# A chunk inverse ahead of the attention, with twelve gate projections between its steps

## The chip, the cores and the metric

The kernel runs on one core of a Trainium2 chip. The metric is the device time of the whole program in microseconds (us), here the median of three runs. Engines are named as the profile names them: PE is TensorE's matmul, PEld its weight load, DVE is VectorE, ACT is ScalarE, POOL is GpSimd, SP is SyncE, which here only issues transfers.

## The reference

One layer of a streaming encoder on 1,024 tokens of 1,024 channels in float32: token mixing, cross attention into 256 memory tokens, and a retrieval over 16,384 single-neuron experts, each with a residual. What the change touches is the token mixing:

```
proj = rmsnorm(x) @ w_in          # sb_q, sb_k, sb_v | g_q, g_k, g_v | g_z | g_b, g_a | gate_sb, gate_gdn
o_sb = stick_breaking_attention(sb_q, sb_k, sb_v)            # 8 heads x 64, causal
q, k, v = silu(causal_dwconv([g_q, g_k, g_v]));  q, k = l2norm(q), l2norm(k)
A  = strict_lower(beta * (k k^T) * decay)                    # per chunk and head, 4 heads x 128
u, w = (I + A)^-1 [beta v, beta k exp(g)]                    # the chunk inverse
for each chunk: v' = u - w S;  o = (q S) + (q k^T * decay) v';  S = decayed S + k^T v'
o_g = rmsnorm(o) * silu(g_z)
merged = sigmoid(gate_sb) * (o_sb @ w_sb_up) + sigmoid(gate_gdn) * (o_g @ w_gdn_up)
out = merged @ w_mix_out
```

The retrieval takes 128 experts per token: their rows of `peer_u` (dot products with the token), a GELU with gates, and the weighted sum of their rows of `peer_v`.

## The kernel before, in words

The tokens go through in three groups of 256, 384 and 384, called g0, g1 and g2 here. `token_mixing(g)`, the cross attention and the routing (which picks the experts) follow each other for each group; g2's routing is followed by dense products over all experts (`dense_h`, line 975), which replace the retrieval for the last tokens. The retrieval of the earlier tokens runs beside all of that from g1 on: line 778 (POOL) gathers 128 expert rows of 4 KB per instruction by an indirect transfer into a `row` buffer; for `peer_u` line 794 (DVE) multiplies the rows by the tokens and sums them (called a u reduce here; a second instruction reads out the sum), for `peer_v` either line 823 (PE, groups of eight small matmuls into `ac`) or line 83 (DVE, into `y`) adds them up.

The order on each engine is set when the program is built, by a scheduler that goes by its own estimate of times, under the dependencies, the buffers and the lifetimes of the memory pools; the engines then work through their lists strictly in order. Code written one after the other is thus interleaved where buffers allow.

Inside `token_mixing` (lines 440 to 550) the steps before are: the norm; twelve projections of 128 columns each for g_q, g_k, g_v with their short convolution (`gc` buffers); beta and decay; SiLU (line 487); l2norm of q and k (line 493 on PE and line 83 `gc<-gc,sq` on DVE); twelve projections for the attention ("SB projections", into `qT`, `kT` and, transposed, `vN`); the attention itself, `stick`, in blocks of 128 queries and 128 keys, two generators (heads 0 to 3 and 4 to 7) in turn; twenty gate projections, whose sigmoid goes to DRAM; the chunk inverse; the scan over the chunks; then the output projections (first DVE line 571, `gr`).

Every projection (`proj`, lines 226 to 240) loads a 512 KB tile of weights, splits it in two parts (ACT line 77 `wh<-raw`, DVE line 89 `wl<-raw,wh`) and runs 24 matmuls (line 223) into one of two PSUM buffers `pj`. One block pair of the attention (called a pair here: one generator, one key block) has one ACT instruction `sh<-z` (line 80), by which pairs can be counted; g0 has 6 pairs, g1 24, g2 42. `pool.tensor_tensor(after, ...)` is line 295.

A chunk's inverse (`Chunk.inverse`, lines 373 to 415) first prepares A (lines 326 to 365, up to `X` in line 377), then doubles diagonal blocks over six levels, each a chain PE (line 379/393/395), ACT (`K`, `E`), DVE or ACT (`X`, line 399), with masks by POOL (line 370). The two or three chunks of a group run in turn. Chunk 0 uses the PSUM tile `z`, chunk 1 `acc`, chunk 2 the two `pj` buffers, the same that the projections use.

The pools: `pn`/`ta` hold `kT`, `vN`, `qT` and the attention's buffers; `d2` holds the inverse's. They are opened one after the other, so what is opened second reuses the memory of the first.

Of the kernel before, what the change touches and what calls it, by code (L numbers as in the profile page):

```python
# [8 lines left out]
F32 = mybir.dt.float32  # L9
# [11 lines left out]
P = 128  # L21
D = 1024
# [29 lines left out]
def block_kernel(ctx: ExitStack, tc: tile.TileContext, x_t, mem_t, gains, cst, sel, eye, w_in, conv, a_log,  # L52
# [22 lines left out]
    # ---- small helpers  # L75
# [9 lines left out]
    def split(hi, lo, src, scale=1.0, eng=vec):  # L85
        """src * scale = hi + lo, both in the tensor engine's fast float32 format."""
        copy(hi, src, scale)
        if scale == 1.0:
            eng.tensor_tensor(lo, src, hi, op=OP.subtract)  # L89
        else:  # L90
            stt(lo, src, scale, hi, OP.mult, OP.subtract)
# [10 lines left out]
    def acc_keep(o, lhsT, rhs, start):  # L102
        """Matmul onto a bank that is read between its accumulation steps."""
        pe.matmul(o, lhsT=lhsT, rhs=rhs, start=start, stop=True, skip_group_check=True)
# [13 lines left out]
    def mix(a, b, ratio):  # L118
        """Steps of a and b in turn, ratio of a for each of b."""
# [21 lines left out]
    # ---- constants  # L141
# [43 lines left out]
    # ---- scratch in DRAM  # L185
# [15 lines left out]
    # ---- building blocks  # L201
    def norm_t(hi, lo, tmp, xs, gi, n, keep=None):
        """RMSNorm over the partitions and tiles of xs(k), [P, n] each, split in two parts."""
# [22 lines left out]
    def proj(w, col0, ncol, hi, lo, n, kt=KD, share=0):  # L226
        """Yields (tile index, product) for each 128 columns of w, transposed: [columns, tokens]. GpSimd splits
        every share-th tile of w."""
# [35 lines left out]
    # ---- stick-breaking attention of one 128-query block, four heads at a time, keys on partitions  # L264
    def stick(tmp, kT, vN, qT, sbo, e, qb, t0):
# [4 lines left out]
        for kb in range(qb, -1, -1):  # L270
# [6 lines left out]
            # softplus; for large z the logarithm is z itself  # L277
# [26 lines left out]
    # ---- gated delta net over one 128-token chunk, four heads together  # L304
    class Chunk:
# [67 lines left out]
        def inverse(self):  # L373
            """Inverse of (I + A) by doubling of diagonal blocks, and its transpose; AT holds -A transposed."""
# [26 lines left out]
            # keys and values with tokens on partitions  # L401
# [15 lines left out]
        def scan(self, S, S2, o):  # L417
            """Recurrence over chunks."""
# [17 lines left out]
    def token_mixing(g, t0, T, x1_where, result):  # L436
# [3 lines left out]
        with ExitStack() as eo:  # L440
# [11 lines left out]
            # gated delta net: projections, short convolution  # L452
# [9 lines left out]
            # beta and decay logits  # L462
# [35 lines left out]
            yield  # L498
            with ExitStack() as es:
# [21 lines left out]
                if not last:  # L521
                    sp.dma_start(k_sc[:, :, t0:t1], kT[:, :, t0:t1])
                    sp.dma_start(v_sc[:, t0 // P:t1 // P], vN[:, t0 // P:t1 // P])
                for qb in range(t0 // P, t1 // P):
                    run(*[stick(tmp, kT, vN, qT, sbo, e, qb, t0) for e in range(2)])

            oT = qkv[0]
            with ExitStack() as es:
                tmp = open_pool(f"d2{g}", 2, where=es)
                # output gate and branch gates wait in DRAM  # L530
                n = 0
                for o, m in ((O_Z, 512), (O_GS, 2048)):
                    for i, ps in proj(w_in, o, m, xh, xl, T, share=SH_Z):
                        e = po.tile([P, T], F32, name="ev", bufs=2)
                        sigmoid(e, ps)
                        if o == O_Z:
                            vec.tensor_mul(e, e, ps)
                        sp.dma_start(gate_sc[g, n, :, :T], e)
                        n += 1
                chunks = []  # L540
                for c in range(NB):
                    cc = slice(c * P, (c + 1) * P)
                    chunks.append(Chunk(tmp, c, qkv[0][:, :, cc], qkv[1][:, :, cc], qkv[2][:, :, cc], bT[:, cc], gT[:, cc]))
                run(*[ch.inverse() for ch in chunks])
                for c, ch in enumerate(chunks):
                    cur = chunk_no[0] % 2
                    chunk_no[0] += 1
                    ch.scan(state[cur], state[1 - cur], oT[:, :, c * P:(c + 1) * P])
# [86 lines left out]
    def routing(g, x1, t0, T, where, kept=None):  # L635
        """Returns the pool that choose() goes on with, and by block the best scores and keys."""
# [62 lines left out]
    def choose(tmp, tv, ti):  # L699
        """The sixteen best sums per head of one 128-token block. A pair (a, b) of ranks can be among them  # L700
        only with (a + 1) * (b + 1) <= 16: a < 4 with all b, or b < 4."""
# [21 lines left out]
        # gate: softmax over the chosen sixteen (the first is the largest)  # L723
# [7 lines left out]
        # position -> ranks -> expert  # L731
# [43 lines left out]
    # ---- retrieval by gathering expert rows  # L775
# [6 lines left out]
    def retrieve_u(blk, keep):  # L782
        """Expert activations of one block; tokens on partitions, one slot per gather."""
# [25 lines left out]
    def retrieve_v(blk, keep):  # L809
        """Weighted sum of expert rows, residual and final norm; slots on partitions, one token per gather."""  # L810
# [22 lines left out]
    def retrieve_y(blk, keep):  # L833
        """The same with tokens on partitions, one slot per gather."""
# [26 lines left out]
    def finish(y, ps, r0):  # L861
        """Final norm of 64 tokens, 32 w + p: quarter d of the channels of token (w, p) is y[32 d + p, w]."""
# [11 lines left out]
    # ---- retrieval by dense products over all experts, for the last tokens  # L874
    def choose_t(p2, tv, ti):
        """Keys and gates of one block with the slots on partitions."""
# [8 lines left out]
    def spread(px_, sel3, b):  # L885
        """Gates as a matrix: g_sc[c, i, r, t] is the gate of token 32 * c + t for expert 128 * r + i, zero if not
# [236 lines left out]
```

## Time and profile before

| | |
|---|---|
| median of three runs | 3813.43 us (3813.3 to 3814.75) |
| span of the profiled execution | 3821.6 us, 8.2 us (0.2%) above that median |
| PE, PEld busy | 3402.2 us (89%), 2852.3 us (75%) |
| DVE, ACT, POOL busy | 2852.1 us (75%), 1624.2 us (43%), 1993.3 us (52%) |
| indirect gathers (queue q0) | 671 MB, 49.4% of sixteen DMA engines' span |
| other transfers (queue q1) | 426 MB, 36.4% |

Busy times overlap between the engines. A matmul's end is modelled, so a PE that is busy throughout need not be at its peak; PEld, the weight loads beside it, is read together with it. The profile gives no time of its own for the profiled execution beside the span; the span is taken as that time.

### The profile page before, as it was taken

What the parts mean: (1) busy time and instruction counts of PE and PEld (TensorE: products, weight loads), DVE (VectorE), ACT (ScalarE), POOL (GpSimd) and SP (SyncE); (2) the same over time, 40 slices, a digit from 0 to 9 for tenths busy, and PEclk for the clock granted to TensorE, in tenths of its full rate; (3) what the DMA queues carried; (4) which work ended last, traced back from release to release, by engine and by line L of the source; (5) the groups of instructions that cost most, each with busy time, mean ns of one, the idle gap of its engine ahead of it and who ended that gap; (6) DMA issues with size and microseconds to landing.
All of it is one profiled execution on the core that took longest, in us unless ns stands there. A gap on an engine that the chain in (4) does not pass through costs nothing. (4 is left out here: it accounts for less than half of the span.)

```text
span 3821.6 us, 56994 instructions
## 1 busy us (share of the span) xinstructions
PE 3402.2 (89%) x20621; PEld 2852.3 (75%) x20621; DVE 2852.1 (75%) x5650; ACT 1624.2 (43%) x2992; POOL 1993.3 (52%) x1611
## 2 busy tenths in 40 slices
PE   7998977898889987999978899989769999999995
PEld 6888866787767765767766667878758888888884
DVE  6445699886566799427896667998767888887886
ACT  5754543664313333545523233556633333333333
POOL 1010007666754546467686455788964545544553
PEclk9999988998989988999979899999969999999997
DMA  6537539987899998989878989998999999999996
GB/s 163 147 92 210 151 110 316 332 293 235 290 353 300 347 335 282 307 301 305 263 248 288 345 301 341 305 315 275 325 316 330 340 339 347 339 327 321 360 386 236
DMA packets 745796, 1100.56 MB, mean 288 GB/s; under 512 B 42149, under 2 KB 554533, under 8 KB 742441
## 3 DMA queue, kind: packets, MB, share of 16 engines
q0 software_dynamic: 184320, 671.17, 49.4%
q1 hardware_dynamic: 561192, 425.73, 36.4%
q8 instruction: 163, 2.67, 0.3%
q14 instruction: 121, 0.98, 0.1%
HBM read 1036.60 MB, written 60.16 MB: 287 GB/s over the span
## 5 line engine op out<-in xcount | busy, mean ns | idle before, releaser
L778 POOL DMA_INDIRECT row<-in_peer_u_dram,ix x640 | 818.7, 1279 | 525.5 <-DVE y L83 146.9
L794 DVE CUSTOM_DVE_ANT_0 row<-row,xs 128x1024 f32<-128x1024 f32 x640 | 818.8, 1288 | 123.5 <-DMA row<-in_peer_u_dram,ix 100.9
L223 PE MATMUL pj<-xhi,wh 128*128 128x384 f32 (+1 forms) x1912 | 636.3, 333 | 52.9 <-ACT xhi L77 20.6
L223 PE MATMUL pj<-xhi,wl 128*128 128x384 f32 (+1 forms) x1912 | 637.0, 333 | 26.6 <-POOL wl L89 16.6
L89 DVE TENSOR_TENSOR wl<-raw,wh 128x1024 fp32r<-128x1024 f32 (+1 forms) x420 | 489.9, 1167 | 227.5 <-ACT wh L77 203.7
L778 POOL DMA_INDIRECT row<-in_peer_v_dram,it x384 | 448.6, 1168 | 358.3 <-PE ac L823 169.0
L223 PE MATMUL pj<-xlo,wh 128*128 128x384 f32 (+1 forms) x1912 | 621.4, 327 | 6.4 <-DVE xlo L89 6.4
L77 ACT ACTIVATE wh<-raw 128x1024 fp32r<-128x1024 f32 (+1 forms) x447 | 449.8, 1007 | 276.2 <-PE pj L223 176.5
L778 POOL DMA_INDIRECT row<-in_peer_v_dram,ix x256 | 352.0, 1375 | 346.7 <-DVE y L83 171.9
L223 PE MATMUL pj<-xh,wh 128*128 128x384 f32 x1152 | 399.9, 347 | 44.6 <-ACT h L80 41.6
L223 PEld LDWEIGHTS pj<-xhi,wh 128*128 128x128 f32 x1912 | 371.1, 194 | 89.6 <-ACT xhi L77 26.8
L223 PEld LDWEIGHTS pj<-xhi,wl 128*128 128x128 f32 x1912 | 370.9, 194 | 65.2 <-POOL wl L89 19.5
L223 PE MATMUL pj<-xh,wl 128*128 128x384 f32 x1152 | 398.8, 346 | 4.3 <-POOL wl L89 3.4
L223 PE MATMUL pj<-xl,wh 128*128 128x384 f32 x1152 | 393.1, 342 | 0.0
L223 PEld LDWEIGHTS pj<-xlo,wh 128*128 128x128 f32 x1912 | 369.4, 194 | 23.2 <-issue 10.6
L83 DVE SCALAR_TENSOR_TENSOR y<-row,hh,y 128x1024 f32<-128x1024 f32 x256 | 329.1, 1285 | 14.6 <-DMA row<-in_peer_v_dram,ix 13.1
L823 PE MATMUL ac<-row,sb 128*32 128x256 f32 x3072 | 267.0, 408 | 51.1 <-DMA row<-in_peer_v_dram,it 45.9
L89 POOL TENSOR_TENSOR wl<-raw,wh 128x1024 fp32r<-128x1024 f32 x27 | 66.0, 2443 | 428.1 <-DVE one L758 330.5
L77 ACT ACTIVATE vh<-vr 128x1024 fp32r<-128x1024 f32 x128 | 134.8, 1058 | 322.9 <-PE pj L975 311.6
L223 PEld LDWEIGHTS pj<-xh,wh 128*128 128x128 f32 x1152 | 220.3, 191 | 66.3 <-ACT h L80 56.9
L223 PEld LDWEIGHTS pj<-xh,wl 128*128 128x128 f32 x1152 | 220.7, 192 | 20.0 <-POOL wl L89 4.2
L89 DVE TENSOR_TENSOR vl<-vr,vh 128x1024 fp32r<-128x1024 f32 x128 | 156.5, 1223 | 90.7 <-ACT vh L77 79.3
(453 smaller groups left out, 6583.7 us busy)
## 6 DMA issues: line engine op xcount, KB each, us to landing
raw<-in_w_in_dram SPq DMA_DIRECT2D x132, 512.0 KB
raw<-in_peer_ut_dram SPq DMA_DIRECT2D x128, 512.0 KB
vr<-in_peer_v_dram SPq DMA_DIRECT2D x128, 512.0 KB
raw<-in_w_pq_dram SPq DMA_DIRECT2D x48, 512.0 KB
g_sc<-st SPq DMA_DIRECT2D x12, 2048.0 KB
gm<-g_sc SPq DMA_DIRECT2D x32, 768.0 KB
raw<-in_w_mix_dram SPq DMA_DIRECT2D x24, 512.0 KB
raw<-in_w_cq_dram SPq DMA_DIRECT2D x24, 512.0 KB
```

The lines of the kernel that those rows point to most:

```text
L77: return act.activation(o, i, AF.Copy, scale=scale)
L83: return vec.scalar_tensor_tensor(out=o, in0=a, scalar=s, in1=b, op0=op0, op1=op1)
L89: eng.tensor_tensor(lo, src, hi, op=OP.subtract)
L223: pe.matmul(ps, lhsT=a[:, k], rhs=b[:, k], start=i == 0, stop=i == 3 * kt - 1)
L778: pool.indirect_dma_start(out=t, out_offset=None, in_=src, in_offset=bass.IndirectOffsetOnAxis(ap=index, axis=0))
L794: vec.tensor_tensor_reduce(out=t, in0=t, in1=xs, scale=1.0, scalar=0.0, op0=OP.mult, op1=OP.add, accum_out=hh[:, j:j + 1])
L823: pe.matmul(ac[32 * d:32 * d + 32, 256 * w:256 * w + 256], lhsT=sb[:, j], rhs=t[:, 256 * d:256 * d + 256], start=j == 0, stop=j == 31)
```

## The change

The pool `d2` is now opened ahead of `pn`/`ta`. In it the inverse's steps are dealt out in turn with the first twelve gate projections (four for g_z, eight for gate_sb), one after each round of the chunks' steps; then comes the scan. After it `pn`/`ta` are opened, the SB projections run, and the attention, with the other eight gate projections (gate_gdn), one after every second round of the two generators. All arithmetic is the same, and every engine has the same number of instructions but for one. The new lines stand at 499 to 527 and 552 to 561 of the changed kernel; lines behind them are 13 higher (the u reduce is line 807 there, the gather 791).

```diff
+            oT = qkv[0]
+            def gates(spans):
+                for n, o, m in spans:
+                    for i, ps in proj(w_in, o, m, xh, xl, T, share=SH_Z):
+                        e = po.tile([P, T], F32, name="ev", bufs=2)
+                        sigmoid(e, ps)
+                        if o == O_Z:
+                            vec.tensor_mul(e, e, ps)
+                        sp.dma_start(gate_sc[g, n + i, :, :T], e)
+                        yield
+            with ExitStack() as es:
+                tmp = open_pool(f"d2{g}", 2, where=es)
...
+                early = gates(((0, O_Z, 512), (4, O_GS, D)))
+                for _ in steps(*[ch.inverse() for ch in chunks]):
+                    next(early, None)
+                for _ in early:
+                    pass
+                for c, ch in enumerate(chunks):
...
+                    ch.scan(state[cur], state[1 - cur], oT[:, :, c * P:(c + 1) * P])
             with ExitStack() as es:
                 pn = open_pool(f"pn{g}", 1, where=es)
                 tmp = open_pool(f"ta{g}", 2, where=es)
...
+                late = gates(((12, O_GG, D),))
+                n = 0
                 for qb in range(t0 // P, t1 // P):
-                    run(*[stick(tmp, kT, vN, qT, sbo, e, qb, t0) for e in range(2)])
-            oT = qkv[0]
-            with ExitStack() as es:
-                tmp = open_pool(f"d2{g}", 2, where=es)
-                n = 0
-                for o, m in ((O_Z, 512), (O_GS, 2048)):
-                    for i, ps in proj(w_in, o, m, xh, xl, T, share=SH_Z):
...
+                    for _ in steps(*[stick(tmp, kT, vN, qT, sbo, e, qb, t0) for e in range(2)]):
                         n += 1
-                run(*[ch.inverse() for ch in chunks])
...
+                        if n % 2 == 0:
+                            next(late, None)
+                for _ in late:
+                    pass
```

**ScalarE (ACT) during the l2norm of g1.** The rows are a piece of the difference, `-` before, `+` after. `sq` are the norm's square roots, `qT`, `kT` the results of SB projections, `ev` that of a gate projection, `wh` the split of a weight tile.

```order
-L80 ACTIVATE sq<-sq 128x384 x3
-L77 ACTIVATE qT<-pj 128x384
-L77 ACTIVATE wh<-raw 128x1024
+L80 ACTIVATE sq<-sq 128x384 x2
+L80 ACTIVATE ev<-pj 128x384
+L77 ACTIVATE wh<-raw 128x1024
+L80 ACTIVATE sq<-sq 128x384
+L80 ACTIVATE ev<-ev 128x384 x2
 L80 ACTIVATE sq<-gc_5777 128x384
```

The SB projections have left this place, and gate projections stand in theirs, but fewer: the order of PE has the twelve SB projections of g1 there before, and three to four gate projections after (the other eight or nine stand among the inverse's levels, behind chunk 2's steps in the `pj` buffers).

**VectorE (DVE) in the inverse's levels of g1, before.** `X0`, `X1`, `X2` are the copies that end one step of chunk 0, 1 and 2; line 794 is the u reduce (its second row reads out the sum).

```order
L399 COPY X0_8607<-z_8595 128x512
L794 ISA row_12146,hh_12014<-row_12146,xs_12012 128x1024
L794 ISA hh_12014 128x1
L794 ISA row_12155,hh_12014<-row_12155,xs_12012 128x1024
L794 ISA hh_12014 128x1
L399 COPY X1_8621<-acc_8609 128x512
L794 ISA row_12164,hh_12014<-row_12164,xs_12012 128x1024
L794 ISA hh_12014 128x1
L399 COPY X2_8635<-pj_8623 128x512
```

The same place after, chunk 0 to chunk 1:

```order
L399 COPY X0_7194<-z_7182 128x512
L807 ISA row_11941,hh_11616<-row_11941,xs_11614 128x1024
L807 ISA hh_11616 128x1
L807 ISA row_11944,hh_11616<-row_11944,xs_11614 128x1024
L807 ISA hh_11616 128x1
L807 ISA row_11947,hh_11616<-row_11947,xs_11614 128x1024
L807 ISA hh_11616 128x1
L89 TENSOR_TENSOR wl_7227<-raw_7224,wh_7226 128x1024
L807 ISA row_11950,hh_11616<-row_11950,xs_11614 128x1024
L807 ISA hh_11616 128x1
L399 COPY X1_7208<-acc_7196 128x512
```

Between two steps of the inverse stand more u reduces than before, and the split of a gate's weight tile. From the last `X` of line 377 to the last product with `vb` (line 410) the order has 16 u reduces before and 40 after; from the first SiLU product (line 487) to that last `X` it has 56 after.

**ScalarE behind the scan of g1, before and after.** `gc0<-...` is the scan's output; `h` and `oh` belong to the output projections.

```order
L77 ACTIVATE gc0_5777<-pj_9047 128x4x128
L80 ACTIVATE h_9080<-gc0_5777 128x384
L77 ACTIVATE wh_9183<-raw_9181 128x512
L80 ACTIVATE h_9084<-acc_9082,epsc_100 128x384
L80 ACTIVATE h_9093<-gc0_5777 128x384
```

```order
L77 ACTIVATE gc0_5777<-pj_7778 128x4x128
L77 ACTIVATE qT_7799<-pj_7806 128x384
L77 ACTIVATE wh_7866<-raw_7864 128x1024
L77 ACTIVATE qT_7799<-pj_7838 128x384
L77 ACTIVATE wh_7898<-raw_7896 128x1024
L77 ACTIVATE qT_7799<-pj_7870 128x384
```

Before, the output projections follow the scan; after, the twelve SB projections do, with nothing of the token mixing beside them, then the attention, in which the eight late gates all stand within the first sixteen pairs or so.

## Rows read from the trace of the kernel before

**Rows 1.** The page: a costly group (count, busy us, mean ns, idle).

```profile
L794 DVE CUSTOM_DVE_ANT_0 row<-row,xs 128x1024 f32<-128x1024 f32 x640 | 818.8, 1288 | 123.5 <-DMA row<-in_peer_u_dram,ix 100.9
```

**Rows 2.** Busy times in stretches of the span (first line: columns).

```profile
core 0: us, PE busy (x) PEld busy (x) DVE busy (x) ACT busy (x) POOL busy (x), PEclk, DMA share, GB/s
651.00:715.00 64.00, 53.21 (x273) 50.35 (x272) 50.48 (x79) 35.33 (x66) 49.82 (x29) 0.91 0.93 314
715.00:893.00 178.00, 176.50 (x979) 145.30 (x978) 146.80 (x217) 112.85 (x199) 104.52 (x80) 1.00 0.87 290
893.00:937.00 44.00, 33.94 (x229) 25.64 (x228) 28.92 (x54) 9.94 (x28) 31.59 (x27) 0.71 0.71 231
937.00:1007.00 70.00, 70.00 (x610) 59.31 (x609) 36.59 (x51) 27.84 (x50) 55.44 (x46) 0.99 0.74 243
1007.00:1038.00 31.00, 26.10 (x204) 18.89 (x195) 19.34 (x41) 6.93 (x13) 22.72 (x20) 0.89 0.90 314
1320.00:1460.00 140.00, 110.86 (x702) 83.98 (x700) 140.00 (x640) 46.46 (x78) 68.14 (x60) 0.82 0.94 322
1553.00:1640.00 87.00, 86.58 (x632) 63.59 (x631) 30.98 (x39) 50.95 (x102) 44.67 (x39) 1.00 0.93 306
1740.00:1880.00 140.00, 139.29 (x782) 111.74 (x781) 118.80 (x170) 81.71 (x147) 98.15 (x74) 1.00 0.90 294
1880.00:1937.00 57.00, 45.77 (x173) 29.67 (x172) 51.19 (x75) 20.27 (x34) 47.50 (x36) 0.73 0.77 251
1937.00:1982.00 45.00, 29.86 (x162) 25.34 (x161) 43.57 (x73) 10.19 (x28) 39.45 (x29) 0.73 0.77 250
1982.00:2057.00 75.00, 63.38 (x516) 60.03 (x516) 54.06 (x80) 29.18 (x51) 59.98 (x46) 0.91 0.72 227
2057.00:2082.00 25.00, 18.89 (x152) 13.82 (x152) 15.63 (x32) 6.89 (x13) 17.81 (x16) 0.93 0.94 329
2440.00:2841.00 401.00, 325.15 (x2028) 288.14 (x2027) 337.10 (x891) 233.87 (x573) 333.84 (x316) 0.87 0.87 303
2841.00:3776.00 935.00, 904.49 (x4402) 795.86 (x4403) 777.38 (x910) 323.37 (x438) 457.32 (x331) 1.00 1.00 341
```

**Rows 3.** Groups on ScalarE, stretch 715 to 893.

```profile
L80 ACT ACTIVATE sh<-z 128x512 f32<-128x512 f32 x24 | 14.3, 596 | 25.9 <-PE z L104 25.8
```

**Rows 4.** Groups on ScalarE, stretch 1740 to 1880.

```profile
L80 ACT ACTIVATE sh<-z 128x512 f32<-128x512 f32 x20 | 11.9, 597 | 26.3 <-PE z L104 26.3
...
L80 ACT ACTIVATE ev<-pj 128x384 f32<-128x384 f32 x15 | 7.3, 486 | 4.4 <-PE pj L223 4.2
```

**Rows 5.** Groups on ScalarE, stretch 1880 to 1937.

```profile
L80 ACT ACTIVATE sh<-z 128x512 f32<-128x512 f32 x9 | 5.3, 593 | 14.1 <-PE z L104 14.1
```

**Rows 6.** Timeline of PE in one gate projection (start, duration).

```profile
1809.08 0.34 PE L223 MATMUL pj<-xhi,wh 128*128 128x384 f32 x1
...
1812.03 0.34 PE L223 MATMUL pj<-xlo,wh 128*128 128x384 f32 x1
```

**Rows 7.** Groups on VectorE, stretch 651 to 715.

```profile
L89 DVE TENSOR_TENSOR wl<-raw,wh 128x1024 fp32r<-128x1024 f32 x9 | 10.9, 1215 | 2.9 <-ACT wh L77 2.5 <-issue 0.4
L487 DVE TENSOR_TENSOR gc<-gc,sq 128x384 f32<-128x384 f32 x12 | 6.4, 548 | 0.8 <-ACT sq L80 0.8
L794 DVE DVE_READ_ACCUMULATOR2_ANT hh<- 128x1 f32 x26 | 2.0, 77 | 0.0
```

**Rows 8.** Groups on GpSimd, stretch 567 to 1038: the gathers.

```profile
L778 POOL DMA_INDIRECT row<-in_peer_u_dram,ix x168 | 222.2, 1323 | 104.1 <-DVE hh L794 54.6 <-issue 31.3 <-DMA ix<-id_sc 7.9
L778 POOL DMA_INDIRECT row<-in_peer_v_dram,it x39 | 49.0, 1257 | 30.5 <-DVE hh L794 21.5 <-issue 6.9 <-DVE bg L329 0.6
```

**Rows 9.** Line 794, 893 to 1030: its waits (us, times).

```profile
  DMA row<-in_peer_u_dram,ix: 36.6, 17
```

**Rows 10.** Line 370 (inverse, GpSimd), 157 to 247: ns min/median/max.

```profile
L370 POOL TENSOR_TENSOR D<-A,cs x8: 1270/1282/2304, 186.5 to 225.3; 128x512 f32<-128x512 f32 x8
```

**Rows 11.** Line 370, 1937 to 2057, the same columns.

```profile
L370 POOL TENSOR_TENSOR D<-A,cs x12: 1274/1294/1584, 1960.5 to 2031.4; 128x512 f32<-128x512 f32 x12
```

More of the change, by code (lines that the diff above doesn't have):

```diff
@@ L498, in token_mixing @@
             yield
+            oT = qkv[0]
[10 more added lines that the diff above has]
+                tmp = open_pool(f"d2{g}", 2, where=es)
+                chunks = []
+                for c in range(NB):
+                    cc = slice(c * P, (c + 1) * P)
+                    chunks.append(Chunk(tmp, c, qkv[0][:, :, cc], qkv[1][:, :, cc], qkv[2][:, :, cc], bT[:, cc], gT[:, cc]))
+                early = gates(((0, O_Z, 512), (4, O_GS, D)))
[4 more added lines that the diff above has]
+                for c, ch in enumerate(chunks):
+                    cur = chunk_no[0] % 2
+                    chunk_no[0] += 1
+                    ch.scan(state[cur], state[1 - cur], oT[:, :, c * P:(c + 1) * P])
             with ExitStack() as es:
@@ L523, in token_mixing @@
                     sp.dma_start(v_sc[:, t0 // P:t1 // P], vN[:, t0 // P:t1 // P])
+                late = gates(((12, O_GG, D),))
+                n = 0
                 for qb in range(t0 // P, t1 // P):
-                    run(*[stick(tmp, kT, vN, qT, sbo, e, qb, t0) for e in range(2)])
-            oT = qkv[0]
-            with ExitStack() as es:
-                tmp = open_pool(f"d2{g}", 2, where=es)
-                n = 0
-                for o, m in ((O_Z, 512), (O_GS, 2048)):
-                    for i, ps in proj(w_in, o, m, xh, xl, T, share=SH_Z):
[L534 to L538, printed above, removed]
-                        n += 1
[L540 to L543, printed above, removed]
-                run(*[ch.inverse() for ch in chunks])
[L545 to L548, printed above, removed]
+                    for _ in steps(*[stick(tmp, kT, vN, qT, sbo, e, qb, t0) for e in range(2)]):
+                        n += 1
+                        if n % 2 == 0:
+                            next(late, None)
+                for _ in late:
+                    pass
             if g == 0:
```

## The prediction

> **What bounds the kernel now.** I read the stretches of the span first, cut where a step's own lines begin and end [rows 2], then the groups on single engines, then the order of both programs. No engine binds the whole span; the reader should compare stretches. In the attention of g1 (715 to 893) PE is busy 176.5 of 178 us at full clock; so it is from 1740 to 1880 in g2, where gate projections stand between the pairs. From 1880 to 1937, where the gates are used up, PE is busy 45.8 of 57 at a granted clock of 0.73. The inverse's preparation (893 to 937, 1937 to 1982) is a waiting stretch: PE 33.9 of 44 and 29.9 of 45, clock 0.71 and 0.73. Its levels have PE busy 70.0 of 70 and 63.4 of 75. SiLU and l2norm of g2 (1553 to 1640) are PE-bound, 86.6 of 87, since the SB projections fill them. From 2841 on the dense products hold PE at 904.5 of 935. Beside all this the gathers and the u reduces run as a second stream, and who gets ahead in it matters later: DVE is busy all of 1320 to 1460.
>
> So both old covers were good ones: the SB projections hid SiLU and l2norm, the gates hid the attention's waits. The change gives each cover another place to fill.
>
> **The unit prices.** The matmuls of a gate projection start 2.95/17 = 0.1735 us apart [rows 6], so one projection of 24 is 4.16 us of PE, and twelve are 50. A u reduce is 1.288 [rows 1] and its read-out 0.077 [rows 7], together 1.37. A pair of the attention without gates is 57/9 = 6.3 us [rows 2, 5]; with 15 gates among 20 pairs it is 140/20 = 7.0 [rows 2, 4], so a gate there costs (140 - 20 x 6.3)/15 = 0.9 us of time for 4.16 of PE: mostly, but not wholly, hidden. In g1 a pair with gates is 178/24 = 7.4 [rows 2, 3].
>
> **g0.** It has no gathers beside it, its gates are free to run ahead of the inverse (two chunks, no step in the `pj` buffers), and PE is busy there throughout. I put it at 0, with 8 us to either side.
>
> **g1, step by step.** Before, from the end of the convolution to `gr`: 64 + 178 + 44 + 70 + 31 = 387 us [rows 2].
> (1) SiLU, l2norm and preparation now run in one piece. In the order 56 u reduces stand on DVE between the first SiLU product and the last `X` of line 377: 76 us. Beside them stand 4 splits (4.9), 12 SiLU products (6.6) [rows 7], 27 other wide products at about 0.6 (16 to 18) and small ones (about 4): 110 on DVE. I take 114, against 64 + 44 = 108 before. If DVE waited for rows as it did in 893 to 1030 (36.6 us, [rows 9]) it would be 140; if the reduces didn't delay the chain, 90.
> (2) The levels, with nine gates: 70 + 9 x 4.16 = 107 if nothing is hidden. PEld, which can't be stretched by waits, is busy 59.3 of 70 [rows 2], so about 11 us of PE time are free: 96. Bounds 70 and 107. Each step now also waits for four to five u reduces on DVE where two stood.
> (3) The scan and what lies behind it: 31, as before.
> (4) The SB projections, which need the memory of the closed pool, begin after the scan, and nothing of the token mixing stands beside them. PE alone needs 50; the stretch that held them in g2 took 87. I take 58, nearer to PE's price as no chain runs through them. The loads of the old `kT`, `vN` also move behind the scan on SP's queue, but aren't read before the attention: nothing, as long as (4) lasts.
> (5) The attention: 24 x 6.3 + 8 x 0.9 = 158, against 178. The bounds on the pair are 7.4 (nothing gained) and 4.1, what PE would need if the 19 or so gates of before are taken out of its busy time (176.5 - 79)/24.
> Sum 114 + 96 + 31 + 58 + 158 = 457, **+70**.
>
> **g2.** Before: 87 + 297 + 45 + 75 + 25 = 529, of which 297 is 1640 to 1937 [rows 2]. After: SiLU, l2norm and preparation 90. This is 132 before, less 33 for eight projections' worth of PE that have left a PE-bound stretch, less 9 for preparation that the order has ahead of l2norm (bounds 70 and 117; the u reduces hardly stand there, as the `peer_v` rows go through PE). Levels 75 + 37 - 15 = 97 (PEld 60.0 of 75; bounds 75 and 112). Scan 25, SB projections 58, attention 42 x 6.3 + 8 x 0.9 = 272. Sum 542, **+13**.
>
> **Given back.** A longer token mixing lets the gathers get ahead; the order shows by how much. When g2's convolution is reached, 22 fewer u reduces remain for the routing stretch that DVE fills (140 of 140): 22 x 1.37 = 30 at most, 25 taken, since some routing is not DVE's. Between g2's routing and the first dense row 26 fewer gathered rows are worked off; DVE is busy 337 of those 401 us, so between 0 and 36, 15 taken. In the dense rows PE's floor is 904.5 of 935: at most 30, and 10 taken, since fewer `y` rows stand in the early ones. Together **-50**.
>
> **Sum.** 70 + 13 - 50 = +33 on the span of 3821.6: 3854.6. That span is 8.2 above the median of the runs, so the runs should show 3846. The likeliest case alone covers 3825 to 3870.
>
> **The rivals.**
> *Faster: the gates fit the inverse's gaps.* If PE's idle time and its low clock in preparation and levels take the gates entirely, the levels last 70 and 75, as before, and 48 comes off: -15, or 3798. It decides below 160 us for the two stretches of levels together (I say 193). For it: PE idles 10 and 15 us in the preparations. Against it: PE's busy row in g1's levels is already 70 of 70, and the gates can't pass chunk 2's steps, which hold the same `pj` buffers.
> *Nothing or faster: all is given back.* If the three later stretches are DVE-bound to the last microsecond, they return 30 + 36 + 30 = 96, the net is -13 and the time 3800. For it: DVE is at 140 of 140 in one of them. Against: 401 us hold 64 us of idle DVE in the second, and the third can give 30 only if `y` rows were what held PE.
> *Slower: the gathers set the pace.* They went at 471/(168 + 39) = 2.28 us each [rows 8]. At the first dense row 29 more of them are due; at that pace +66, less 10 in the dense rows: 3869. Against: between stages DMA's share is only 0.71 to 0.77 in the inverse's stretches [rows 2], so a faster pace is to be had there.
> *Slower: the attention doesn't shrink.* If PE is not what holds it and the gates were free, 178 and 294 stay for (5): 20 + 22 more, 3888. For it: ScalarE waits for PE's `z` 25.8 of 178 us even so [rows 3], and PEld is busy only 145 of 178. Against: [rows 5], 6.3 us per pair at a lower clock.
> The Trainium skill says in Perfetto Trace Analysis, Identifying the Most-Contended Engine, that matmul busy time is a poor measure and the weight loads' busy share the better one. By that rule PE has 18% left in g1's attention, which is this rival; the trace agrees in that the 87 us of g2's SiLU show 86.6 of matmul and 63.6 of weight loads.
> *Slower: GpSimd's masks and the u reduces shut each other out.* In g0 one mask of line 370 took 2.30 instead of 1.28 us [rows 10]. If all 14 and 21 masks of the two level stretches did so, now that more u reduces stand beside them: 35 x 1.02 = 36 more, 3882. Against: in g2, with u reduces beside them, twelve of them had a median of 1.29 and a maximum of 1.58 [rows 11].
> The Trainium skill's SBUF — State Buffer, Who interferes with whom, states such a lock for a DVE instruction with two SBUF inputs against a GpSimd instruction that reads SBUF; by it 3882 could come true, and the trace bears it out in single instructions only.
>
> **How the numbers follow.** Chances: the likeliest case 0.45, gates in the gaps 0.17, all given back 0.14, the gathers' pace 0.14, the attention's pace 0.06, the masks 0.04. The predicted time is that of the likeliest, 3846. The range 3790 to 3888 leaves out the lower part of the first two rivals and the upper part of the last two. A difference under 0.2% (7.6 us) is about what a measurement of this kernel can't tell from none. Faster: 0.13 from the gaps, 0.09 from what is given back, 0.03 from the low bounds of (1) and (5): 0.25. Within 0.2%: 0.13, the rest of these two and the edge of the likeliest. Slower: 0.62.
>
> **What the profile after would show.** (1) No stretch of SB projections before the scan; the last `X` of line 377 in g1 about 114 us after the convolution. (2) Levels of 96 and 97 us, with `ev<-pj` among them. (4) A stretch of twelve line-223 tiles behind each scan, 58 us, with PE and little else. (5) Pairs at 6.3 to 6.6 us, ScalarE's `sh<-z` 24 in 158. The first dense row some 40 us later than 2841, its rows at PE's floor. Wrong would be: levels near 70 (the first rival), pairs at 7 or 5, a dense stretch that starts no later, or rows that DVE waits for at every u reduce.

## The result, and the profile after

The changed kernel takes 3922.34 us in the median of four runs (3907.41 to 3932.62), the kernel before 3814.09 beside it: a ratio of 1.0279, interval 1.0248 to 1.0311. It is **slower by 2.8%**, or 108 us. Forecast were +33 and a range that ended at 3888: the sign was right, the size was not. The first profile is of its fastest execution (span 3905.6); a second one of the same kernel, in the experiments, has a span of 3938.9.

The stages of the span, cut at the first or last instruction of their lines and rounded to whole us, show where the time went. `gr` is the first product of line 583 (596 in the changed kernel). The forecast column is the prediction's sum.

| stage | before, us | forecast change | after, first profile | after, second |
|---|---|---|---|---|
| start to `gr` of g0 | 315 | 0 | +15 | +14 |
| to the end of g1's convolution | 337 | 0 | +19 | +20 |
| to `gr` of g1 | 386 | +70 | +57 | +68 |
| to the end of g2's convolution | 516 | -25 | -31 | -23 |
| to `gr` of g2 | 528 | +13 | +20 | +32 |
| to the first dense row | 758 | -15 | +13 | +15 |
| dense rows | 928 | -10 | -4 | -3 |
| end | 54 | 0 | -5 | -6 |
| sum | 3822 | +33 | +84 | +117 |

The kernel after, in stretches that answer to [rows 2] (first line: columns):

```profile
core 0: us, PE busy (x) PEld busy (x) DVE busy (x) ACT busy (x) POOL busy (x), PEclk, DMA share, GB/s
74.00:147.00 73.00, 65.94 (x456) 59.97 (x454) 37.04 (x63) 51.75 (x133) 7.52 (x7) 0.88 0.52 137
584.00:686.00 102.00, 62.51 (x286) 59.88 (x285) 97.92 (x174) 34.76 (x55) 78.20 (x53) 0.78 0.94 313
686.00:785.00 99.00, 61.10 (x242) 47.11 (x243) 92.00 (x160) 38.98 (x86) 84.54 (x58) 0.66 0.84 289
785.00:894.00 109.00, 98.35 (x724) 93.98 (x724) 81.00 (x111) 44.76 (x80) 81.71 (x61) 0.94 0.85 282
894.00:916.00 22.00, 19.13 (x172) 15.79 (x171) 11.34 (x25) 3.45 (x7) 17.02 (x16) 1.00 0.98 356
916.00:974.00 58.00, 58.00 (x385) 49.15 (x384) 24.82 (x33) 18.20 (x27) 32.14 (x28) 1.00 1.07 367
974.00:1129.00 155.00, 145.30 (x913) 99.62 (x912) 86.88 (x127) 84.57 (x149) 81.61 (x70) 0.99 0.71 235
1614.00:1692.00 78.00, 73.20 (x592) 46.64 (x585) 32.73 (x64) 44.69 (x104) 49.36 (x48) 0.96 0.92 322
1692.00:1803.00 111.00, 107.89 (x853) 95.42 (x853) 72.57 (x103) 48.11 (x90) 87.06 (x70) 1.00 0.93 323
1803.00:1823.00 20.00, 15.97 (x102) 14.60 (x102) 17.14 (x37) 2.39 (x4) 16.72 (x11) 0.91 0.86 285
1823.00:1899.00 76.00, 58.92 (x307) 57.24 (x307) 48.92 (x71) 19.00 (x28) 48.97 (x33) 0.87 0.97 328
1899.00:2162.00 263.00, 232.51 (x1336) 152.00 (x1334) 194.21 (x287) 126.73 (x222) 205.93 (x162) 0.91 0.85 282
2162.00:2933.00 771.00, 636.11 (x3849) 550.04 (x3849) 592.88 (x1577) 353.31 (x801) 486.70 (x458) 0.89 0.86 292
2933.00:3857.00 924.00, 895.12 (x4370) 789.14 (x4371) 749.49 (x873) 326.28 (x440) 399.23 (x303) 1.00 0.97 331
```

Read against the steps of the prediction: g1's (1) took 99 (114 said), (2) 109 (96), (4) 58 (58), (3) and (5) together 177 (189); in g2 78 (90), 111 (97), 76 (58) and 283 (297). The SB projections stand alone behind the scan, as said. What was not said is that the attention of g2, once it has few gates, leaves PE more room: PEld is busy 152 of 263 us, where it was 112 of 140 while gates stood between the pairs [rows 2]. Two stages that the sum had at nothing, the first two of the table, lost 34 us, and the stage before the dense rows lost where a gain was forecast.

ScalarE's wait for line 295 in the attention of g2: before (1650 to 1937), after (1911 to 2151), and in the variant below that keeps the old order, mix_old_order (1673 to 1972). Columns: who waited for whom, us in total, times, longest.

```profile
ACT l L80 <- POOL after L295: 30.0, 21, 5.3
```

```profile
ACT l L80 <- POOL after L295: 54.9, 28, 4.8
```

```profile
ACT l L80 <- POOL after L295: 73.2, 23, 7.9
```

On GpSimd the attention's running sum (line 295) stands in one list with the gathers: after, 120 gathers stand among its 30 sums, and only 6 of the sums found GpSimd idle. ScalarE waits for the sum, since the buffer `l` is free again only then. With gates between the pairs PE has work meanwhile; with fewer, more of the wait lies open. How much of it is time lost is for the experiments on that sum below to say. The attention's 42 pairs, before and after:

```profile
1650.00:1937.00 287.00, 275.06 (x1632) 194.87 (x1625) 194.72 (x277) 140.67 (x248) 200.27 (x159) 0.95 0.86 283
```

```profile
1911.00:2151.00 240.00, 213.58 (x1219) 136.91 (x1219) 175.94 (x257) 111.49 (x193) 193.03 (x150) 0.90 0.84 277
```

### The profile page after: what moved, and what is told of

The parts are those of the page before. It is cut to its first block, busy times and chain, and to the rows that moved or that the text cites. A ratio compares the mean times of both kernels' runs of the same rounds, so it can differ in the third digit from the quotient of the medians.

```text
span 3905.6 us, 57005 instructions
## 1 busy us (share of the span) xinstructions
PE 3414.0 (87%) x20621; PEld 2867.8 (73%) x20621; DVE 2836.8 (73%) x5650; ACT 1623.9 (42%) x2993; POOL 1965.2 (50%) x1611
## 5 line engine op out<-in xcount | busy, mean ns | idle before, releaser
L223 PE MATMUL pj<-xhi,wh 128*128 128x384 f32 (+1 forms) x1912 | 640.7, 335 | 60.1 <-ACT xhi L77 19.5
L791 POOL DMA_INDIRECT row<-in_peer_v_dram,it x384 | 437.6, 1140 | 339.0 <-PE ac L836 151.5
L791 POOL DMA_INDIRECT row<-in_peer_v_dram,ix x256 | 332.1, 1297 | 421.6 <-DVE y L83 181.1
L223 PEld LDWEIGHTS pj<-xhi,wl 128*128 128x128 f32 x1912 | 377.3, 197 | 59.4 <-POOL wl L89 18.1
L836 PE MATMUL ac<-row,sb 128*32 128x256 f32 x3072 | 256.1, 404 | 34.8 <-DMA row<-in_peer_v_dram,it 33.4
```

The source lines that it names most:

```text
L223: pe.matmul(ps, lhsT=a[:, k], rhs=b[:, k], start=i == 0, stop=i == 3 * kt - 1)
L791: pool.indirect_dma_start(out=t, out_offset=None, in_=src, in_offset=bass.IndirectOffsetOnAxis(ap=index, axis=0))
L836: pe.matmul(ac[32 * d:32 * d + 32, 256 * w:256 * w + 256], lhsT=sb[:, j], rhs=t[:, 256 * d:256 * d + 256], start=j == 0, stop=j == 31)
```

## The experiments

Each was timed in five rounds against the kernel before on the same chip; the name in brackets is that of the run. The medians of before beside them were 3819.6 (again, only_g0, mix_old_order, sb_ahead), 3814.9 (late20, sum_on_vector, gates_swapped, few_rows), 3825.6 (early20, before_sum_vec, sb_ahead_sum_vec, only_g2) and 3816.1 (only_g1, swap_middle, swap_split). Ratios are given with their intervals.

**The change itself, again** (again). 

> The changed kernel as it is, for a second profile and more runs: 3907 to 3933 us again. The first profile was of its fastest execution. If the spread between executions comes from one place (theory: the gathers' transfers, which run at the DMA limit there), the second profile shows it as one or two longer stretches; rival: it is a little of everything with the clock.


3937.21 us, 1.0303 (1.0279 to 1.0327), a little above what was expected. The table's last column: the second profile's extra 33 us come in three of its stages, +11, +8 and +12, all of them token mixing or what stands between one group's and the next, none in the dense rows. Which engine's luck that is stays open; the kernel before had runs from 3802.5 to 3834.6 as well.

**The change in g0 alone** (only_g0). The groups not named take the old lines.
```diff
+            if g in (0,):
+                with ExitStack() as es:
+                    tmp = open_pool(f"d2{g}", 2, where=es)
...
+            else:
+                with ExitStack() as es:
+                    pn = open_pool(f"pn{g}", 1, where=es)
...
```


> The change in g0 alone, g1 and g2 as before. Theory (a delay in token mixing is carried to the end, since nothing later waits less for it): about +15 to +20, 3830 to 3834. Rival (what g0 loses is taken back by the later stretches, which are bound by other things): 3814, no change.


3863.36 us, 1.0110 (1.0089 to 1.0131). `gr` of g0 comes 15 us later, that of g1 15 and that of g2 19. That looks like the theory's delay carried on, but it is not one: at the end of g2's convolution only 5 us are left, and g2's token mixing, which the edit doesn't touch, adds 14. Then the way to the first dense row takes 783 us instead of 758. The loss is twice what was expected, and more than half of it arises 2,000 us behind the edit.

**Only the dealing out, the attention ahead as before** (mix_old_order; shown against the kernel before).
```diff
-                    run(*[stick(tmp, kT, vN, qT, sbo, e, qb, t0) for e in range(2)])
+                    for _ in steps(*[stick(tmp, kT, vN, qT, sbo, e, qb, t0) for e in range(2)]):
+                        n += 1
+                        if n % 2 == 0:
+                            next(late, None)
...
-                run(*[ch.inverse() for ch in chunks])
...
+                for _ in steps(*[ch.inverse() for ch in chunks]):
+                    next(early, None)
...
```


> The attention ahead of the inverse as before, the gates dealt out as in the change: 8 between attention steps, 12 among the inverse's. Theory (order costs, dealing out doesn't): the levels get 38 and 36 us longer as in the changed kernel, the attention 36 and 50 shorter: 3795 to 3815. Rival (gates among the inverse's steps cost by themselves): 3850 or more.


3924.66 us, 1.0275 (1.0251 to 1.0299). The theory falls and the rival holds: with no change of order the loss is as large. It lies elsewhere, though. g1's token mixing takes 389 us for 386, with its attention 15 us shorter and its levels some 30 longer, and g2's takes 587 for 528; then the way to the first dense row takes 786 for 758. The attention of g2, with 8 gates instead of 20, got longer, 299 us against 287, and waits 73.2 us for line 295. Its stretch, and that of the preparation behind it:

```profile
1673.00:1972.00 299.00, 253.60 (x1342) 163.42 (x1342) 202.66 (x299) 114.43 (x203) 218.70 (x174) 0.81 0.82 277
1972.00:2031.00 59.00, 41.53 (x235) 37.09 (x236) 50.12 (x88) 19.11 (x42) 50.10 (x34) 0.79 0.77 262
```

PE's clock fell to 0.81 where it was 0.95 over the same pairs before. So twelve gates more had cost that attention of g2 nothing, and they are not free where they went: from the attention's first pair to `gr` g2 takes 487 us, against 432.

**Only the order, all twenty gates with the attention** (late20).
```diff
-                early = gates(((0, O_Z, 512), (4, O_GS, D)))
-                for _ in steps(*[ch.inverse() for ch in chunks]):
-                    next(early, None)
...
+                run(*[ch.inverse() for ch in chunks])
...
-                late = gates(((12, O_GG, D),))
+                late = gates(((0, O_Z, 512), (4, O_GS, 2 * D)))
...
-                        if n % 2 == 0:
+                        if n % 1 == 0:
...
```


> The inverse ahead of the attention, but with no gates among its steps: all twenty gates between attention steps, one after every round. Theory (dealing gates into the inverse costs about 60 of the 110 us): 3850 to 3870. Rival (the order costs, through the exposed SB projections): 3920 to 3940.


3966.56 us, 1.0398 (1.0371 to 1.0425): worse than the whole change, beyond what the rival said. The levels are back at 73 us in g1 (89 in g2), but in g1 with idle PE; the attention with its gates takes 171 and 268 us (159 and 287 before), and the SB projections are exposed besides. The levels of g1 and the attention with the way to `gr`:

```profile
789.00:862.00 73.00, 59.80 (x431) 56.43 (x431) 60.85 (x83) 24.60 (x41) 64.33 (x47) 0.87 0.74 233
962.00:1148.00 186.00, 172.63 (x1060) 136.99 (x1056) 83.63 (x114) 100.72 (x179) 63.25 (x54) 0.96 0.58 185
```

So the parts don't add: dealing out alone +105, order alone +152, both +108 to +118. One reading is that the order takes a cover away and the dealing out, in that order, puts a part of it back.

**All twenty gates among the inverse's steps** (early20). The gates of the attention go to the inverse.
```diff
-                early = gates(((0, O_Z, 512), (4, O_GS, D)))
+                early = gates(((0, O_Z, 512), (4, O_GS, 2 * D)))
...
-                late = gates(((12, O_GG, D),))
...
```


> The changed order with all twenty gates among the inverse's steps, none in the attention. Theory (a gate among the levels costs nearly its 4.16 us, one in the attention about 1): g1 and g2 together 30 to 50 us longer, 3955 to 3980. Rival (the inverse has room for them, and the attention without any gets shorter by as much): 3900 to 3935.


3913.97 us, 1.0230 (1.0203 to 1.0257), no more than the change itself and inside the rival's range. The theory falls, but not in its first half. Of the eight gates moved, five to six more stand in the levels (13 and 14 projections there, against 8 in the change), the rest behind them. They made the levels 21 and 17 us longer, 3.9 and 2.8 us a gate. The attention of g1 with its way to `gr` is 26 shorter without its gates, that of g2 equal:

```profile
783.00:913.00 130.00, 119.28 (x840) 115.64 (x839) 91.60 (x124) 57.34 (x102) 84.65 (x64) 0.96 0.86 285
1005.00:1134.00 129.00, 112.76 (x767) 68.24 (x767) 84.02 (x129) 65.81 (x117) 96.33 (x81) 0.98 0.85 292
1705.00:1833.00 128.00, 124.56 (x926) 115.01 (x925) 94.68 (x133) 57.99 (x110) 100.55 (x78) 1.00 0.97 339
1924.00:2186.00 262.00, 220.02 (x1218) 131.82 (x1216) 180.00 (x273) 109.91 (x190) 204.71 (x165) 0.84 0.81 274
```

So a gate among the levels costs most of its 4.16 us. The change's eight had cost all of it in g1: its levels take 73 us without gates (late20) and 109 with eight, 4.5 us a gate. In the old order eight cost 3.3 to 3.8 each (levels of 100 and 101 in mix_old_order, 70 and 75 before). What the theory missed is g1's attention, where eight gates less gave back 3 us each and not 1.

**The SB projections ahead of the inverse again** (sb_ahead), keys and values parked in DRAM, the rest as changed.
```diff
+                qs = pn.tile([P, 4, T], F32, name="qT")
                 for i, ps in proj(w_in, O_SB, 1536, xh, xl, T, share=SH_S):
...
+                    if i < 8:
+                        sp.dma_start(k_sc[:, i - 4, t0:t1], e)
...
+                        sp.dma_start(v_sc[:, t0 // P:t1 // P, (i - 8) * P:(i - 7) * P],
+                                     e2.rearrange("p (b c) -> p b c", c=P))
...
+                    sp.dma_start(kT, k_sc[:, :, :t1])
+                    sp.dma_start(vN, v_sc[:, :t1 // P])
...
```


> Inverse ahead of the attention with the same 12 and 8 gates, but the SB projections stand ahead of the inverse again; their keys and values are parked in DRAM and loaded for the attention. Theory (the exposed SB projections are the cost: 37, 58 and 76 us in the changed kernel, less some 10 us each for the loads): 3922 - 130 = about 3790 to 3815. Rival (the u reduces and gates among the inverse's steps are the cost): it stays above 3880.


3911.67 us, 1.0230 (1.0206 to 1.0253). The theory falls, and the rival's range holds: the exposed projections are not most of the cost. g1's token mixing behind the convolution takes 410 us (443 in the change, 386 before): there the exposed projections cost 33. g2's takes 558 against 548 and 560: there they cost nothing, for with them SiLU to the last `X` of line 377 takes 141 us with PE busy throughout, against 78 without. The keys' and values' way through DRAM is in these times too, and its price wasn't told apart.

**Line 295's sum on VectorE.**
```diff
-                pool.tensor_tensor(after, after, l, op=OP.add)
+                vec.tensor_tensor(after, after, l, op=OP.add)
```
In the changed kernel (sum_on_vector): 

> The changed kernel with line 295's running sum of the attention on VectorE instead of GpSimd. Theory (without gates to fill it the attention waits for that sum, which stands behind gathers on GpSimd's queue: 55 us of waits in g2): the attention of g2 gets 20 to 40 us shorter, of g1 up to 20; 3870 to 3905. Rival (PE or the u reduces on VectorE hold the attention): 3920 to 3950, the wait moves to VectorE.


3871.15 us, 1.0158 (1.0132 to 1.0184): 51 us below the change's first median and 66 below its second. That is inside what the theory said. The attention of g2 shrinks from 240 to 218 us with the clock at 0.98 instead of 0.90, g2's token mixing to 521, less than the 528 of before; g1's gains only 5, and the way to the first dense row is 18 shorter. The wait of 54.9 us is gone but for 13.4 us on VectorE's sum.

```profile
1910.00:2128.00 218.00, 198.69 (x1224) 128.19 (x1222) 174.28 (x285) 110.27 (x193) 149.25 (x120) 0.98 0.88 304
```

In the kernel before (before_sum_vec): 

> The kernel before with line 295's running sum on VectorE. Theory (gates between the attention's steps already fill the wait for that sum: 10 us of waits in g1, 30 in g2, and any new plan costs 14 to 23): 3800 to 3840. Rival (the sum on VectorE helps by 50 to 60 us wherever it is done, as it did in the changed kernel): 3755 to 3770.


3873.16 us, 1.0128 (1.0103 to 1.0152): slower, beyond both. The attention of g2, which has its gates, takes 299 us for 287, and the way from `gr` of g2 to the first dense row 802 for 758. Why isn't shown. ScalarE's wait for the sum fell from 30.0 to 12.6 us, and VectorE is busy only 209 of the 299 us; but GpSimd's gathers wait 59.4 us for u reduces there, where they waited 19.5 before. The first lines of waits from 1643 to 1942:

```profile
POOL row L778 <- DVE hh L794: 59.4, 41, 4.5
ACT sh L80 <- PE z L104: 58.1, 30, 3.7
```

With the SB projections ahead of the inverse (sb_ahead_sum_vec): 

> The variant with the SB projections ahead of the inverse, and line 295 on VectorE. Theory (the exposed projections of g1 and the wait for the sum are separate costs that add): 3912 - 45 to 60 = 3850 to 3870, near the kernel before plus a new plan. Rival (they are one and the same idle time of PE): 3890 to 3915.


3856.41 us, 1.0084 (1.0051 to 1.0116): 55 us below sb_ahead, the theory's sum, but not by its reason. ScalarE's wait for the sum in g2's attention fell by 53 us (1891 to 2139 in sb_ahead, 1891 to 2131 here):

```profile
ACT l L80 <- POOL after L295: 70.8, 28, 7.3
```

```profile
ACT l L80 <- DVE after L295: 17.7, 10, 4.4
```

Yet that attention is only 8 us shorter and g2's token mixing 1 longer; 37 of the 55 come on the way to the first dense row (747 us for 785), where that sum isn't done. So the wait's total is not what its removal is worth. This is the best version with the inverse ahead; none beat the kernel before.

**The change in one other group alone** (only_g2, only_g1). g2: 

> The change in g2 alone. Theory (g2's own cost of 20 to 32 us and a new plan's 14 to 23): 3850 to 3870, with g0 and g1 as before. Rival (the loss in g2 was handed down from g0 and g1 through where the gathers stand): 3815 to 3840.


3881.45 us, 1.0153 (1.0124 to 1.0182), more than expected. g2's token mixing takes 568 us, +40 where +20 to +32 was seen behind the changed g0 and g1, and the way to the first dense row +25.
g1: 

> The change in g1 alone. Theory (the parts add: g0 alone gave +44, g2 alone +56 to +67, each with one new plan of some 20 in it, the whole +108 to +118): g1 gives +57 - 25 for what comes back behind it, and the plan: 3860 to 3875. Rival (g1's loss needs g0's in front of it): 3830 to 3845.


3897.47 us, 1.0212 (1.0195 to 1.0229): more than expected. The convolution of g1 takes 100 us for 88, with the 45 u reduces of the change in place of 36, though no code ahead of it changed. The mixing takes 437 (+50), and 9 of the delay come back before g2's `gr`, not 25.
In the medians the three lose 44, 81 and 56 us, 181 together, and the whole change 108 to 118. They don't add up, but each has the price of a new plan in it, which the next paragraph finds. At `gr` of g2 they are 19, 56 and 42 late, 117 together; the whole change is 80 late there in its first profile and 110 in its second, so up to that point a regain between the groups isn't shown.

**Neutral edits of the kernel before** (gates_swapped, swap_middle, swap_split). The gates are written in another order, here with the four of g_z last.
```diff
-                for o, m in ((O_Z, 512), (O_GS, 2048)):
...
+                for _ in gates(((4, O_GS, 2 * D), (0, O_Z, 512))):
+                    pass
...
```


> The kernel before with one neutral edit: the twenty gate projections are written in another order (the four for g_z last), so that the scheduler plans anew. Every variant so far, even the one with the change in g0 alone, lost 13 to 28 us between g2's output projections and the first dense row. Theory (that stretch was well met by the old plan, and any new plan meets it worse): 3835 to 3845, the loss behind g2's output projections. Rival (it comes from the gathers standing further ahead): 3814 to 3820, no loss there.


3837.77 us, 1.0060 (1.0038 to 1.0081). `gr` of g2 comes 1 us later than before, the first dense row 15. That 1 us is a sum of larger shifts: g1's convolution ends 11 us later, g1's mixing is 23 shorter, g2's 17 longer. The way from `gr` of g2 to the first dense row, before and with the edit:

```profile
2082.00:2840.00 758.00, 656.07 (x4083) 548.89 (x4083) 600.57 (x1592) 354.39 (x803) 523.62 (x485) 0.91 0.92 315
```

```profile
2083.00:2855.00 772.00, 640.83 (x4050) 545.02 (x4049) 603.59 (x1602) 352.57 (x801) 528.53 (x491) 0.91 0.92 314
```

> A second neutral edit of the kernel before: the g_z gates between the two groups of eight. Theory (a new plan costs 14 to 25 us behind g2's output projections, whatever the edit): 3830 to 3845. Rival (that was the chance of one plan; others come out as before or better): 3795 to 3822.


3824.45 us, 1.0026 (1.0011 to 1.0040); the stretch takes 761 us.


> A third neutral edit: two g_z gates first, then eight, the other two of g_z, eight. Theory as for the second: 3830 to 3845. Rival: 3795 to 3822.


3836.18 us, 1.0055 (1.0039 to 1.0070); the stretch takes 773 us.
So in these three edits a new plan alone costs 8 to 23 us, with the same work in the same stages. The theory's 14 to 25 was too narrow on the low side: the second edit met neither range and is hardly apart from no change. With the plan alone a single stage got up to 23 us shorter and up to 17 longer, so a stage's shift of that size, in any run here, need not come from its edit.

**Fewer gathers** (few_rows). The kernel leaves out 31 gathers of block 2: one row tile stands for 32, and the matmuls stay.
```diff
-                    t = fetch(peer_v, it[:, c0 + j:c0 + j + 1])
+                    if not (blk == 2 and c0 == 96 and j):
+                        t = fetch(peer_v, it[:, c0 + j:c0 + j + 1])
```


> The kernel before without 31 of the gathers of block 2's peer_v rows (one row tile stands for 32, the matmuls stay). The prediction held that gathers that get ahead shorten the stretch behind g2's routing. Theory now (that stretch is set by its own chain of one-hot steps, and block 7's gathers can't start before its routing): within 10 us of before, 3805 to 3820. Rival (the gathers' pace sets it): 31 x 1.4 to 2.28 less, 3745 to 3770.


3839.06 us, 1.0065 (1.0045 to 1.0085). With 31 gathers less, 0.52 MB each, it is not faster: 24 us above before, over the theory's range and far from the rival's, about where the dearer neutral edits lie, which plan anew as it does. The last `peer_v` gather of block 2 is issued at 2481 instead of 2705, and the first dense row starts at 2863 instead of 2840. In the changed kernel the same can be seen directly; all that GpSimd does from 2620 to 2680 there:

```profile
L916 POOL TENSOR_SCALAR o<-io,sel 128x128 f32<-128x128 f32 x28 | 20.4, 742 | 19.1 <-PE acc L917 18.2 <-ACT sel L77 0.9
L89 POOL TENSOR_TENSOR wl<-raw,wh 128x1024 fp32r<-128x1024 f32 x2 | 4.9, 2428 | 13.9 <-ACT wh L77 13.9
```

No gather for these 60 us, nor at all from 2583 to 2702: those of the blocks before are done, and the next gather waits for the indices (`ix<-id_sc`) that block 7's routing stores. Before, no two gathers in that stretch begin more than 18 us apart. The lead that the longer token mixing gave them ends there.

## Why the prediction was wrong

**Two steps failed, and a third was mis-sized.** The first profile is 51 us over the sum's +33. Of these, 34 lie in the two stages that the sum had at nothing and 28 in what was not given back (22 of 50 came); the chain of g1 and g2 took 6 less than forecast, the end 5 less than before.

The step **"Given back"** failed in its two later terms. Its first, -25, came out at -31 and -23. The second, -15 for 26 fewer gathered rows before the dense part, came out at +13 and +15. The lead was there: 248 gathers were issued in that stretch, 275 before, and it still got longer. few_rows speaks for the reason, that the stretch is not set by the gathers; a gain of 15 hidden there would need a new plan at 39 us, dearer than any of the three neutral ones. Of the sixteen other profiles only three took less for it than the 758 of before (753 with the sum on VectorE, 754 with all gates early, 747 with the SB projections ahead and the sum on VectorE). What does set it stays open; GpSimd's one-hot steps of line 916 waiting for PE, above, are where I would look. The neutral edits alone put 3 to 16 us on it, so +13 may be no more than a new plan. The third, -10, was -4.

The step **"g0 ... I put it at 0"** failed: +15 at its `gr`. Its reason, that PE is busy there throughout, held before and not after. From 74 to 147 the gates stand beside SiLU and l2norm in place of the SB projections, and PE is busy 65.9 of 73 us at a clock of 0.88, where it was busy 80.0 of 83 at 1.00. From 74 to `gr` PE is idle 16 us where it was idle 8, and its busy time is 7 longer. The same stretch before:

```profile
74.00:157.00 83.00, 80.00 (x599) 72.48 (x598) 42.44 (x56) 66.50 (x148) 4.78 (x2) 1.00 0.54 149
```

only_g0 has the same +15, but doesn't show it carried to the end. With this step fell the silent term behind it: the way to the end of g1's convolution, +19. The order had 45 u reduces beside the convolution for 36, nine more at 1.37 us, 12 us on a VectorE that is busy 97.9 of 102; the number stood in the order and was not in the sum. Before, the convolution with 36:

```profile
564.00:652.00 88.00, 60.10 (x291) 57.25 (x290) 85.80 (x154) 30.21 (x46) 65.43 (x46) 0.85 0.97 322
```

How many stand there is a matter of the plan as a whole, and the stretch mostly follows their number: 92 and 93 us with 38 (swap_split, only_g0), 98 to 99 with 41 (gates_swapped, swap_middle, mix_old_order), 100 to 103 with 45 (the change, early20, sum_on_vector, only_g1). The three neutral edits alone put 4 to 11 us there; few_rows and only_g2 keep the 36, and 87 to 88 us.

**The chain of g1 and g2** was right in place and order, and close in its sum: +77 in the first profile (57 and 20), +100 in the second, forecast +83. That the sum is close is partly luck, as its parts were off both ways. (2) was the term mis-sized: 96 and 97 were said, 109 and 111 measured, which are its bounds of 107 and 112 for "nothing is hidden". The 11 and 15 us that it took off for PEld's idle share were not to be had in the change. (1) was 15 and 12 too long. In g1 its 110 us of VectorE's work was right from the first SiLU product (675.7) to the last `X`, 109 us, but the first 10 of them pass before the convolution ends, where the stage was cut. (4) in g2 took 76 for 58, and (3) and (5) together were 12 and 14 shorter than said. The reasons hold only in part. That "nothing of the token mixing stands beside" the SB projections is right in both groups, but their place costs only 33 of the 58 us in g1, by sb_ahead, and nothing in g2. **(5)** priced a pair without gates at 6.3 us, from nine pairs behind the gates; after, the 42 pairs of g2 took 240/42 = 5.7, in mix_old_order 7.1. The wait for line 295, 54.9 and 73.2 us there, was in no step. It is a part of a pair's time, not its measure: taking most of it away made the attention 22 us shorter in the changed kernel, 8 in sb_ahead, and left it 12 longer in the kernel before.

**The rivals.** "The gates fit the inverse's gaps": no; the levels took 109 and 111, and a gate there costs 2.8 to 4.5 us. "All is given back": no. "The gathers set the pace": no (few_rows). "The attention doesn't shrink": no in the change (130 us for 159 and 240 for 287), though g2's doesn't in the old order (299). The masks of line 370 against the u reduces: no; in g1's levels after, with 40 u reduces beside them, eight of them read

```profile
L370 POOL TENSOR_TENSOR D<-A,cs x8: 1268/1296/1482, 788.6 to 862.4; 128x512 f32<-128x512 f32 x8
```

with a median as in [rows 11]. The u reduces are longer there, 1.52 us in the mean against 1.29 over the span [rows 1], as the 17 of g1's levels before were with 1.61.
The Trainium skill's SBUF — State Buffer, Who interferes with whom, has a VectorE instruction with two SBUF inputs contend with a GpSimd instruction that reads SBUF, under an exclusive lock where the order of issue decides which one blocks. So the longer u reduces may be that lock on VectorE's side; no run here tells that apart.

**The range** ended at 3888 since every rival changed one stage. It had no term for a new plan (+8 to +23), none for the two stages that it had at nothing (+34), and took the profile's 8 us above the median for granted, where the change's median lies 17 above its first profile's span. What makes its executions differ by 33 us isn't settled.

## What to carry to other kernels

When a scheduler plans the whole program, an edit has a price before it does anything: time neutral ones first, and put that price, here 8 to 23 us in 3814 for three of them, on every forecast. Filler work belongs where the wait is longest, which is told by who waits for whom with the filler taken out, not by an engine's busy share with it in: twelve of the gates that looked like a load on g2's attention were filling its waits. But the total of such a wait is no forecast of what its removal gives: 41 us of waits less gave 22 us in one kernel, 53 less gave 8 in another. A stream that runs ahead is worth something only up to the next point that it must wait for; look for that point before crediting it.

## What was not expected of the hardware

The same addition of 128 x 512 numbers, moved from GpSimd to VectorE, gained 51 to 66 us in one order and lost some 48 in the other, each with a new plan in it. Over the same 42 attention pairs of g2 PE's granted clock was 0.95 with twenty gates between them, 0.81 with eight in the old order, and 0.90 and 0.98 with eight in the new with the sum on GpSimd and on VectorE.
